# Attention queries and keys produced transposed: the weight slices stand in the array, 256 token columns move

## The chip, the core and the metric

The kernel runs on one core of one Trainium2 chip. Its metric is the device time of one execution in microseconds. The kernel before has a median of 1318.09 us over 3 runs (1317.95 to 1318.52). The engines have the names of the profile: PE is the matrix engine (PEld its weight loads), DVE the vector engine, ACT the scalar engine, POOL the general engine, SP the engine that issues DMAs.

## What is computed

A trunk of two layers over 256 tokens of width 1024, all in float32. Each layer is a half-step feed-forward part, a mixer and another half-step feed-forward part, each with a norm before and a norm after it. The mixer of layer 0 is the dilated attention that the change touches; that of layer 1 is a retention.

```python
def rms_norm(x, g):
    y = x * lax.rsqrt(jnp.mean(x * x, axis=-1, keepdims=True) + NORM_EPS)
    return y * g

# layer 0, mixer
hm = rms_norm(x, g[2])
proj = (h @ w_in).reshape(B, S, N_GROUPS, 3, H_A, DH_A)      # 1024 -> 3 groups x (q, k, v) x 16 heads x 64
for g, (window, dilation) in enumerate(((128, 1), (512, 4), (2048, 16))):
    o, lse = dilated_group(proj[:, :, g, 0], proj[:, :, g, 1], proj[:, :, g, 2], bias_g, dilation, radius)
wts = softmax(stack(lses)); o = einsum('gbsh,gbshd->bshd', wts, stack(outs))
m = o.reshape(B, S, D_A) @ w_out
x = x + rms_norm(m, g[3])
```

## The kernel before

The 256 tokens lie as two tiles t of 128. The normed input is held transposed, as `xh` and `xl` (a rounded half and the remainder), with 8 slices k of 128 features: `xh[:, k, 0:256]` is features by tokens. Each weight is likewise split into `whi` (ACT, L115) and `wlo` (DVE, L116), and a product is three matmuls (`mm3`, L182 to L184): xh by whi, xh by wlo, xl by whi. These tiles have the type fp32r. The norm's gain is multiplied into the weights when they are split; the norm's factor per token, `rstd`, is applied to the products when they leave the accumulator.

Weights stream in: SP loads 1 MB tiles `raw`, ACT and DVE split them into pieces of 1024 columns (two slices k of 512 weight columns) in a ring of six `whi` and six `wlo`, and each piece used up (`done`) triggers the split of a later one. A **unit** is 512 weight columns, so four pieces, and 48 matmuls of 512 columns on PE: for each piece, each of its two k and each t, three matmuls with the 128 tokens as the stationary operand and 512 weight columns moving. Its result, tokens by columns, fills two accumulator banks (`at` in attention; there are six banks in all).

Attention has 18 units in two rounds of 8 heads each (o = 0, 1): q and k of group 0, q and k of group 1, q and k of group 2, then v of the three groups. After a q or k unit ACT copies each accumulator to a tile `nat` and multiplies it by the norm's factor per token, which is one number per partition there (L567; `rq` is -1/8 of `rstd`). The scores need q and k with the head's features on the partitions, so `qk_store` transposes `nat` by four PE transposes of 128 columns per t into a bank `tr` (L624, tile `qkt`; two such banks) and DVE copies that to `qk` (L626 with the token order inside reversed for q, L628 for k). This work is put on the list `pend` and is emitted by `flush` after the second piece of the next unit. Score, softmax and transpose steps of a round wait in `bg`, and `work` emits two of them per piece of the v units.

Outside of two hand-ordered places the order on each engine is set by a scheduler when the program is built. PE, DVE and ACT each take their instructions strictly in that order.

## Time and profile before

| | kernel before |
|---|---|
| median of 3 runs | 1318.09 us |
| the profiled execution | 1317.18 us |
| its span (first to last instruction) | 1315.1 us |
| PE busy | 1298.9 us, 99% |
| PE weight loads busy | 1051.8 us, 80% |
| DVE busy | 864.7 us, 66% |
| ACT busy | 712.1 us, 54% |
| granted PE clock | 0.999 |

The profiled execution is 0.91 us below the median, and 2.1 us of it lie outside the span. A matmul's busy time in the trace is longer than its place in the stream, since the next one starts while it still drains. What a matmul costs is therefore read from start to start.

### The profile page before, as it was taken

How to read it: one execution, taken by the hardware profiler on the slowest of the kernel's cores; microseconds unless marked ns; L12 is line 12 of the kernel's file. 1: busy time of each engine (PE TensorE's matmuls, PEld its weight loads, DVE VectorE, ACT ScalarE, POOL GpSimd, SP SyncE). 2: the span in 40 equal slices, each digit the busy share in tenths (PEclk: the TensorE clock that was granted, in tenths of full speed). 3: DMA queues.
4: the chain of work that ended last, by engine and by line, in shares of the span. 5: the costliest groups of instructions: out<-in, count | busy, mean ns of one | idle time of the engine just before them, and what ended most of it. 6: DMA issues, size and time to landing. Idle time of an engine off the chain costs nothing.

```text
span 1315.1 us, 16640 instructions
## 1 busy us (share of the span) xinstructions
PE 1298.9 (99%) x6326; PEld 1051.8 (80%) x6326; DVE 864.7 (66%) x1541; ACT 712.1 (54%) x1103; POOL 19.4 (1%) x16
## 2 busy tenths in 40 slices
PE   8999999999999999999999999999999999999997
PEld 6878887877887778888888888877888887888886
DVE  5765547678467768765476665588787875766544
ACT  4655444566555658764455654455554545565532
POOL 1000001000000000000000000000000000000000
PEclk9999999999999999999999999999999999999999
DMA  7755467855864346554546555545454545565551
GB/s 214 235 183 192 173 212 183 203 192 147 204 179 158 129 149 227 192 192 173 184 162 227 170 189 192 192 144 185 152 175 145 176 160 192 166 202 183 172 190 64
DMA packets 129691, 235.45 MB, mean 179 GB/s; under 512 B 25019, under 2 KB 41899, under 8 KB 129612
## 3 DMA queue, kind: packets, MB, share of 16 engines
q1 hardware_dynamic: 129468, 234.14, 56.0%
q8 instruction: 49, 0.80, 0.2%
q10 hardware_dynamic: 144, 0.26, 0.1%
q14 instruction: 30, 0.25, 0.1%
HBM read 232.21 MB, written 1.12 MB: 177 GB/s over the span
## 4 chain that ended last, share of the span: by engine, by line
PE 90%; DVE 4%; DMA 3%; ACT 2%; issue 1%; SPq 0%; DVEq 0%; ACTq 0%
PE ac_f L184 12%; PE ac_f L183 12%; PE ac_f L182 12%; PE d_f L182 6%; PE d_f L184 6%; PE d_f L183 6%; PE at L182 5%; PE at L184 5%; PE at L183 5%; PE rt L184 4%; PE rt L183 4%; PE rt L182 4%; PE htr L340 1%; DMA raw<-in_ret_w_in_dram 1%; DMA raw<-in_ffn_w_gate_dram 1%; PE ptt L676 1%
## 5 line engine op out<-in xcount | busy, mean ns | idle before, releaser
L116 DVE SCALAR_TENSOR_TENSOR wlo<-raw,gcol,whi 128x512 fp32r<-128x512 f32 x596 | 417.2, 747 | 191.2 <-ACT whi L115 190.6
L115 ACT ACTIVATE whi<-raw,gcol 128x512 fp32r<-128x512 f32 x596 | 393.8, 715 | 273.2 <-PE ac_f L184 87.1
L110 DVE TENSOR_TENSOR wlo<-raw,whi 128x1024 fp32r<-128x1024 f32 x112 | 137.2, 1225 | 144.9 <-ACT whi L109 144.7
L109 ACT ACTIVATE whi<-raw 128x1024 fp32r<-128x1024 f32 x112 | 118.7, 1060 | 172.2 <-PE d_f L184 103.3
L182 PE MATMUL d_f<-whi,hhf 128*128 128x512 f32 x352 | 140.7, 400 | 0.0
L184 PE MATMUL d_f<-whi,hlf 128*128 128x512 f32 x352 | 138.8, 394 | 0.0
L183 PE MATMUL d_f<-wlo,hhf 128*128 128x512 f32 x352 | 138.2, 393 | 0.0
L182 PE MATMUL at<-whi,xh_f 128*128 128x512 f32 x276 | 111.6, 404 | 0.0
L184 PE MATMUL at<-whi,xl_f 128*128 128x512 f32 x276 | 108.3, 392 | 0.0
L183 PE MATMUL at<-wlo,xh_f 128*128 128x512 f32 x276 | 107.4, 389 | 0.0
L183 PE MATMUL rt<-wlo,xh_f 128*128 128x512 f32 x244 | 97.1, 398 | 0.0
L182 PE MATMUL rt<-whi,xh_f 128*128 128x512 f32 x244 | 96.7, 396 | 0.0
L184 PE MATMUL rt<-whi,xl_f 128*128 128x512 f32 x244 | 96.4, 395 | 0.0
L184 PEld LDWEIGHTS d_f<-whi,hlf 128*128 128x128 f32 x352 | 66.1, 188 | 17.1
L183 PEld LDWEIGHTS d_f<-wlo,hhf 128*128 128x128 f32 x352 | 66.1, 188 | 15.4
L182 PEld LDWEIGHTS d_f<-whi,hhf 128*128 128x128 f32 x352 | 66.1, 188 | 15.1
L182 PE MATMUL ac_f<-whi,xh_in 128*128 128x512 f32 x176 | 70.4, 400 | 2.2 <-ACT whi L115 1.9
L183 PE MATMUL ac_f<-wlo,xh_in 128*128 128x512 f32 x176 | 69.1, 392 | 1.2 <-DVE wlo L116 1.2
L184 PE MATMUL ac_f<-whi,xl_in 128*128 128x512 f32 x176 | 69.3, 394 | 0.0
L184 PE MATMUL ac_f<-whi,xl_at 128*128 128x512 f32 x168 | 66.2, 394 | 0.0
L182 PE MATMUL ac_f<-whi,xh_at 128*128 128x512 f32 x168 | 65.8, 393 | 0.2 <-ACT xh_at L224 0.2
L183 PE MATMUL ac_f<-wlo,xh_at 128*128 128x512 f32 x168 | 65.9, 392 | 0.0
(290 smaller groups left out, 2162.8 us busy)
## 6 DMA issues: line engine op xcount, KB each, us to landing
raw<-in_ffn_w_down_dram SPq DMA_DIRECT2D x44, 1024.0 KB, 4.9
raw<-in_ffn_w_up_dram SPq DMA_DIRECT2D x40, 1024.0 KB, 5.1
raw<-in_ffn_w_gate_dram SPq DMA_DIRECT2D x39, 1024.0 KB, 5.1
raw<-in_attn_w_in_dram SPq DMA_DIRECT2D x36, 1024.0 KB, 5.2
raw<-in_ret_w_in_dram SPq DMA_DIRECT2D x24, 1024.0 KB, 5.4
raw<-in_ret_w_in_dram SPq DMA_DIRECT2D x16, 512.0 KB, 4.6
raw<-in_ret_w_out_dram SPq DMA_DIRECT2D x8, 1024.0 KB, 4.9
raw<-in_ffn_w_gate_dram SPq DMA_DIRECT2D x10, 512.0 KB, 4.1
```

The costliest lines, as they stand in the source:

```text
L109: nc.scalar.activation(hi, raw, AF.Copy)
L110: nc.vector.tensor_tensor(out=lo, in0=raw, in1=hi.bitcast(F32), op=ALU.subtract)
L115: nc.scalar.activation(hi[:, s], raw[:, s], AF.Copy, scale=gc)
L116: nc.vector.scalar_tensor_tensor(out=lo[:, s], in0=raw[:, s], scalar=gc, in1=hi[:, s].bitcast(F32), op0=ALU.mult, op1=ALU.subtract,)
L182: mm(out, xh, wh, start=start, stop=False)
L183: mm(out, xh, wl, start=False, stop=False)
L184: mm(out, xl, wh, start=False, stop=stop)
L340: nc.tensor.transpose(tr[:, k * P : (k + 1) * P], h[:, k * P : (k + 1) * P], self.ident)
L676: self.nc.tensor.transpose(tr[:, c * P : (c + 1) * P], pr[:, c * P : (c + 1) * P], self.ident)
```

## The change

All q and k units but the very first (u = 0), 11 of 12, now run through `unit_t`. There the stationary operand is a slice of 128 weight columns, and the 256 tokens of both tiles move: for each k and each of the four slices c, three matmuls of 256 columns. The result is already transposed, features by tokens, two slices in each bank. The norm's factor is then one number per column, so `rows` builds two tiles `rowsq` and `rowsk` once, with the factor of every token in all partitions: DVE writes the factors on the diagonal of `dg`, PE multiplies by a tile of ones, DVE copies the result out. The accumulators leave through one DVE multiplication per bank by that row (with the token order reversed for q), straight into `qk`. For these units `nat`, the transposes and the copies out of `tr` are gone. The first unit stays as it was, and so do the v units.

```diff
+        self.ones = sb.tile([P, P], F32, name="ones")
+        nc.gpsimd.memset(self.ones, 1.0)
...
+    def unit_t(self, pieces, accs, quota=2):
+        mm = self.nc.tensor.matmul
+        for j, pc in enumerate(pieces):
+            hi, lo = self.ws.get(pc)
+            for kk in range(2):
+                k = 2 * j + kk
+                xh, xl = (z[:, k, 0 : 2 * P] for z in (self.xh, self.xl))
+                for c in range(4):
+                    b, a = divmod(c, 2)
+                    out = accs[b][:, a * 256 : a * 256 + 256]
+                    s = slice(kk * 512 + c * P, kk * 512 + c * P + P)
+                    mm(out, hi[:, s], xh, start=k == 0 and a == 0, stop=False, skip_group_check=True)
+                    mm(out, hi[:, s], xl, start=False, stop=False, skip_group_check=True)
+                    mm(out, lo[:, s], xh, start=False, stop=k == NK - 1, skip_group_check=True)
+            self.ws.done(pc)
+            if j == 1:
+                self.flush()
+            self.work(quota)
+
+    def rows(self, cols, name):
+        nc, sb = self.nc, self.sb
+        d = sb.tile([P, 2, P], F32, tag="dg", name=f"dg_{name}")
+        for t in range(2):
+            nc.vector.tensor_scalar(out=d[:, t, :], in0=self.ident, scalar1=cols[:, t : t + 1], scalar2=None, op0=ALU.mult)
+        tr = self.trb(f"rw_{name}")
+        nc.tensor.matmul(tr[:, : 2 * P], self.ones, d, start=True, stop=True)
+        r = sb.tile([P, 2 * P], F32, tag=f"rows{name}", name=f"rows{name}")
+        nc.vector.tensor_copy(r, tr[:, : 2 * P])
+        return r
...
+                self.pend.append(lambda rq=rq: scales.update(q=self.rows(rq, "q"), k=self.rows(self.rstd, "k")))
...
-                self.unit(pieces, accs, cols=(64, 192) if (kind == "v" and g == 2) else (0, P))
+                if kind == "v":
+                    self.unit(pieces, accs, cols=(64, 192) if g == 2 else (0, P))
+                else:
+                    self.unit_t(pieces, accs)
...
-                for t in range(2):
+                if u:
+                    for b in range(2):
+                        dst = qk[g][:, w, 2 * b : 2 * b + 2, :].rearrange("p a (r i) -> p a r i", r=4)
+                        src = accs[b].rearrange("p (a r i) -> p a r i", a=2, r=4)
+                        sc = scales[kind].rearrange("p (r i) -> p r i", r=4)
+                        if kind == "q":
+                            src, sc = src[:, :, :, ::-1], sc[:, :, ::-1]
+                        nc.vector.tensor_tensor(out=dst, in0=src, in1=sc.unsqueeze(1).to_broadcast([P, 2, 4, 64]), op=ALU.mult)
+                for t in range(2 if u == 0 else 0):
```

On PE, around the start of the second half of a k unit's pieces (unit 3), the kernel before has the transposes of the previous unit (`qkt`) between matmuls of 512 columns:

```order
L184 MATMUL at_3_1_1966<-whi79_1856,xl_f00_1586 128x512
L624 MATMUL qkt20_2007<-ident_79,nat20_1961 128x128 x4
L624 MATMUL qkt21_2013<-ident_79,nat21_1963 128x128 x4
L182 MATMUL at_3_0_1965<-whi80_1884,xh_f00_1585 128x512
L183 MATMUL at_3_0_1965<-wlo80_1885,xh_f00_1585 128x512
L184 MATMUL at_3_0_1965<-whi80_1884,xl_f00_1586 128x512
```

The changed kernel's unit 3 is 96 rows of this kind without a break, here its first ones; the operand named first after the arrow moves, the other one stands in the array:

```order
L340 MATMUL at_3_0_2061<-xh_f00_1587,whi78_1890 128x256
L341 MATMUL at_3_0_2061<-xl_f00_1588,whi78_1890 128x256
L342 MATMUL at_3_0_2061<-xh_f00_1587,wlo78_1891 128x256
L340 MATMUL at_3_0_2061<-xh_f00_1587,whi78_1890 128x256
L341 MATMUL at_3_0_2061<-xl_f00_1588,whi78_1890 128x256
L342 MATMUL at_3_0_2061<-xh_f00_1587,wlo78_1891 128x256
L340 MATMUL at_3_1_2062<-xh_f00_1587,whi78_1890 128x256
L341 MATMUL at_3_1_2062<-xl_f00_1588,whi78_1890 128x256
```

Twice as many matmuls, each half as long, have taken the place of the 48, and the transposes are gone.

On DVE, during unit 1, the kernel before has the splits `wlo` and the copies out of the transposes' banks (`qkt0` of unit 0, `qkt1` of unit 1):

```order
L553 COPY ru_1763<-rut_1760 64x1
L116 SCALAR_TENSOR_TENSOR wlo74_1688<-raw37_1652,gcol_95,whi74_1687 128x512 x2
L116 SCALAR_TENSOR_TENSOR wlo75_1731<-raw37_1652,gcol_95,whi75_1730 128x512 x2
L626 COPY qk00_1767<-qkt00_1814 128x4x128
L626 COPY qk00_1767<-qkt01_1820 128x4x128
L116 SCALAR_TENSOR_TENSOR wlo76_1789<-raw38_1685,gcol_95,whi76_1788 128x512 x2
L116 SCALAR_TENSOR_TENSOR wlo77_1807<-raw38_1685,gcol_95,whi77_1806 128x512 x2
L116 SCALAR_TENSOR_TENSOR wlo78_1839<-raw39_1736,gcol_95,whi78_1838 128x512 x2
L116 SCALAR_TENSOR_TENSOR wlo79_1857<-raw39_1736,gcol_95,whi79_1856 128x512 x2
L628 COPY qk00_1767<-qkt10_1910 128x4x128
```

The changed kernel has, at the same place:

```order
L589 COPY ru_1765<-rut_1762 64x1
L353 TENSOR_SCALAR dg_q_1840<-ident_79,rq_1758 128x128 x2
L116 SCALAR_TENSOR_TENSOR wlo74_1690<-raw37_1654,gcol_97,whi74_1689 128x512 x2
L116 SCALAR_TENSOR_TENSOR wlo75_1733<-raw37_1654,gcol_97,whi75_1732 128x512 x2
L357 COPY rowsq_1845<-rw_q_1843 128x256
L353 TENSOR_SCALAR dg_k_1847<-ident_79,rstd_f00_1589 128x128 x2
L357 COPY rowsk_1852<-rw_k_1850 128x256
L674 COPY qk00_1769<-qkt00_1854 128x4x128
L674 COPY qk00_1769<-qkt01_1860 128x4x128
L612 TENSOR_TENSOR qk00_1769<-at_1_0_1774,rowsk_1852 128x512
L612 TENSOR_TENSOR qk00_1769<-at_1_1_1775,rowsk_1852 128x512
L116 SCALAR_TENSOR_TENSOR wlo76_1803<-raw38_1687,gcol_97,whi76_1802 128x512 x2
```

The four instructions that make the rows and their two copies are new, and unit 1's accumulators now leave on DVE, ahead of the splits `wlo76` and `wlo77` of unit 2's last two pieces, which stand behind them.

## Rows read from the trace of the kernel before

**Rows 1.** The page: busy time by engine; granted PE clock by slice, tenths.

```profile
PE 1298.9 (99%) x6326; PEld 1051.8 (80%) x6326; DVE 864.7 (66%) x1541; ACT 712.1 (54%) x1103; POOL 19.4 (1%) x16
...
PEclk9999999999999999999999999999999999999999
```

**Rows 2.** Waits of PE during attention (204 to 455 us): us, times, longest.

```profile
PE xtr_f L220 <- DVE x L263: 0.3, 1, 0.3
PE rut L548 <- DVE rstd_f L211: 0.3, 1, 0.3
```

**Rows 3.** Windows, each from one block of transposes to the next: two units.

```profile
core 0: us, PE busy (x) PEld busy (x) DVE busy (x) ACT busy (x) POOL busy (x), PEclk, DMA share, GB/s
236.24:248.10 11.86, 11.86 (x59) 9.83 (x58) 4.78 (x9) 6.28 (x10) 0.00 (x0) 1.00 0.69 200
248.10:259.97 11.87, 11.87 (x59) 9.84 (x58) 8.13 (x13) 6.17 (x10) 0.00 (x0) 1.00 0.88 221
```

**Rows 4.** Timeline of PE at the first block of transposes: start us, us, instruction.

```profile
223.13 0.39 PE L183 MATMUL at<-wlo,xh_f 128*128 128x512 f32 x1
223.36 0.39 PE L184 MATMUL at<-whi,xl_f 128*128 128x512 f32 x1
223.59 1.03 PE L624 MATMUL qkt<-ident,nat 128*128 128x128 f32 x8
224.38 0.47 PE L182 MATMUL at<-whi,xh_f 128*128 128x512 f32 x1
224.70 0.39 PE L183 MATMUL at<-wlo,xh_f 128*128 128x512 f32 x1
```

**Rows 5.** Timeline of PE's weight loads at the same place.

```profile
223.14 0.19 PEld L184 LDWEIGHTS at<-whi,xl_f 128*128 128x128 f32 x1
223.37 1.02 PEld L624 LDWEIGHTS qkt<-ident,nat 128*128 128x128 f32 x8
```

**Rows 6.** Timeline of PE: the last three warm-up passes of 128 columns, plain float32.

```profile
4.27 0.50 PE L174 MATMUL warm<-ident 128*128 128x128 f32 x3
4.60 0.25 PE L176 MATMUL gtr<-ident,gr 96*128 96x96 f32 x1
```

**Rows 7.** Loads of line 174, matmuls of line 846: ns min/median/max, first, last start.

```profile
L174 PEld LDWEIGHTS warm<-ident x16: 192/333/338, 1.3 to 4.4; 128*128 128x128 f32 x16
...
L846 PE MATMUL rs<-rc x32: 379/379/483, 889.7 to 1040.6; 128*128 128x256 f32 x32
```

**Rows 8.** Timeline of PE: eight plain float32 passes of 256 columns, the retention scores.

```profile
889.69 1.99 PE L846 MATMUL rs<-rc 128*128 128x256 f32 x8 [0.52 <-ACT rc L837]
```

**Rows 9.** Timelines of PE and PEld: a matmul without a load beside it.

```profile
287.57 0.40 PE L184 MATMUL at<-whi,xl_f 128*128 128x512 f32 x1
...
287.89 0.30 PEld L644 LDWEIGHTS sc<-qk 64*128 64x128 f32 x4 [0.36 <-issue]
```

**Rows 10.** Timeline of PE in a feed-forward down projection.

```profile
159.83 0.40 PE L182 MATMUL d_f<-whi,hhf 128*128 128x512 f32 x1
...
161.23 0.40 PE L182 MATMUL d_f<-whi,hhf 128*128 128x512 f32 x1
```

**Rows 11.** Groups by line: xcount, busy us, mean ns, idle before (first four: attention).

```profile
L116 DVE SCALAR_TENSOR_TENSOR wlo<-raw,gcol,whi 128x512 fp32r<-128x512 f32 x136 | 94.4, 747 | 45.1 <-ACT whi L115 44.9
...
L567 ACT ACTIVATE nat<-at,rq 128x512 f32<-128x512 f32 x12 | 8.1, 683 | 20.4 <-PE at L184 12.8 <-DVE rq L544 7.6
L628 DVE COPY qk<-qkt 128x512 f32<-128x512 f32 x12 | 8.0, 685 | 6.5 <-PE qkt L624 6.5
...
L626 DVE COPY qk<-qkt 128x512 f32<-128x512 f32 x12 | 7.9, 686 | 10.3 <-PE qkt L624 10.3
...
L669 DVE TENSOR_SCALAR pr<-pr,den 128x384 f32<-128x384 f32 x32 | 11.9, 415 | 0.4
L824 DVE TENSOR_TENSOR m<-rt,rtab 128x512 f32<-128x512 f32 x16 | 10.3, 683 | 0.0
L680 DVE COPY PT<-ptt 128x384 f32<-128x384 f32 x16 | 8.8, 551 | 2.5 <-PE ptt L676 2.5
```

More of the change, by code (lines that the diff above doesn't have):

```diff
@@ L535, in attn @@
         rq = ru = None
+        scales = {}
         tasks_o1 = None
```

## The prediction

> **What bounds the kernel now.** I read the page's busy times first. PE is busy 99% of the span at the full granted clock, DVE 66%, ACT 54% [rows 1]. Then the waits of PE: in the whole attention stage it waited twice, 0.3 us each, both before unit 1 is well under way [rows 2]. In the windows from one block of transposes to the next PE is busy in every microsecond, while DVE and ACT idle for a third to a half [rows 3]. So the q and k units cost what PE's stream costs, and what the change adds or takes off PE moves the end by as much; the later stages start when attention is done and are as full of PE.
>
> **What PE's stream costs now.** One q or k unit with a block of transposes takes 11.87 us [rows 3]. The block: the matmul before it starts at 223.36, the second one after it at 224.70; of these 1.34 us two are ordinary matmuls (0.229 each, next sentence), so eight transposes cost 0.88 us, 0.11 each [rows 4]. The other 11.87 - 0.88 = 10.99 us over 48 matmuls make 0.229 us for one of 512 columns, which the starts confirm (223.13 to 223.36) [rows 4].
>
> **The change on PE.** It removes 11 such units with 11 such blocks: 11 x 11.87 = 130.6 us. It adds 11 x 96 = 1056 matmuls of 256 columns, each with a load of its own, at a price p that no row shows: every fp32r matmul of this kernel moves 512 columns. At p nanoseconds they cost 1.056 x p us. So p decides, and I bound it from the nearest rows.
>
> From below. Two rates limit p. Loads: three passes of plain float32 with 128x128 weights, whose loads are 0.19 long as the fp32r ones are (192 at the least; 0.19), follow one another in (4.60 - 4.27) / 3 = 0.11 us [rows 5 to 7]. The stream: eight transposes of 128 float32 columns at 0.11 each, too [rows 4]. Plain float32 passes of 256 columns take (1.99 - 0.38 - 0.10) / 7 = 0.216 (0.38 is the last one's own length, 0.10 the first one's exposed load, 483 less 379) [rows 7, 8]. So float32 doubles with its columns and has some 2 ns that don't. An fp32r matmul has twice these columns in about the same time, 229 against 216, so 256 of them should take what 128 float32 columns take or more: p is not below 109.
>
> From above. The 229 ns are 13 more than the 216 of the float32 pass. Are these 13 per matmul, or do they grow with the columns? If per matmul, p = 109 + 13 = 122. In the down projection the same shape comes every (161.23 - 159.83) / 6 = 0.233 and single starts lie 0.24 apart [rows 10]; with all of that kept per matmul p is 126, and 133 for the worst single ones. If nothing of a load could lie beside a matmul, p would be 0.109 + 0.107 (what a 0.19 load holds up beyond its neighbour, as the first pass of rows 8 shows it) = 216.
>
> What I take. Does the extra come from the load beside the matmul? The one at 287.57 has no load beside it, since the next starts at 287.89, after its place in the stream is over; it is as long as the others or longer (0.40 against 0.39) [rows 4, 9]. So the extra sits in the fp32r stream itself, and a stream's cost goes with its columns. Half of 229, with the 2 ns that don't halve, is **115.5 ns**. That is also between the nearest rows, 111 and 122.
>
> Sum on PE: 1056 x 115.5 ns = 122.0 us against 130.6, so -8.6 us. Then `rows` on PE: two float32 matmuls of 256 columns, two passes each, at 0.216 to 0.23 with the exposed load [rows 8], 0.9 us. And `rut`, which already waits 0.3 us for `rstd` [rows 2], now stands behind 5 short matmuls (0.58 us) instead of 3 long ones (0.69), so it waits 0.1 us longer. **Together -7.6 us**, and in general 1.056 x p - 129.6 (130.6 less 1.0).
>
> **The change off PE.** ACT loses 22 `nat` of 0.68 us, 15 us in all, at no gain: it waits for PE already [rows 11]. DVE loses 22 copies of 0.686 and gets 22 multiplications of 128x512 from an accumulator by a broadcast row; the rotary's have that form and take 0.683 [rows 11]. These now wait for the unit's last matmul with splits queued behind them: the `wlo` of the next unit's third and fourth piece. PE comes to the third piece 48 x 0.1155 = 5.5 us into the unit. DVE needs two multiplications and two splits, 2 x 0.69 + 2 x 0.75 = 2.9 us [rows 11]. The cover is 2.6 us; were it gone, each late microsecond would stand in each of 11 units. Nothing there touches ACT's `whi`, which moves ahead by the missing `nat`. For the rows, DVE does 4 small products, at most 0.415 each, and 2 copies, at most 0.55 [rows 11]. The second row's matmul stands 21 short matmuls (2.4 us) behind the first; DVE's copy and two products between need 1.4. The last transposes of unit 0 wait for the second row's copy (0.55), with four transposes and a matmul (0.55) beside it; so 0 to 0.2 us. SP's queue keeps its order, and POOL gets one memset at the start.
>
> **A rule against it.** The Trainium skill, page "TensorE: Matmul & The Clock Gate", section "The mechanism" with its list of what overlaps, says that a load overlaps matmuls in flight only where its row group differs. Here every load has all 128 rows. By that rule p is 216 and the time 1416.6. The trace speaks against it: the load for the matmul of 223.36 starts at 223.14, beside the one of 223.13, and matmuls still follow each other every 0.229, where 0.229 and a load's 0.107 in a row would make 0.34 [rows 4, 5]. The same page of the Trainium skill, section "Back-to-back issue gap", gives N/2.4 + 2.5 ns for a warm isolated matmul; an estimate by it is 109 ns for N = 256, by which the time would be 1303.6 us, and 216 ns for N = 512, where this trace has 229.
>
> **Rivals.**
> - Both rates run at their floor, p = 109 to 112: 1.056 x 111 - 129.6 = -12.4, so 1305.7 us. For it: the float32 passes of rows 6. Against: fp32r has never been seen at such a pace here.
> - The extra is per matmul, p = 120 to 125: at 122, -0.8, so 1317.3. The transposes' gain is given back by twice as many matmuls, and no change can be measured. For it: no row shows the extra shrink. Against: rows 9.
> - **Slower: the load becomes the bound.** In the stream of now a load of 0.19 ends 0.04 us before its matmul starts; at 0.1155 it must be handed over while its neighbour is still loading. For it: PEld is busy 9.84 of 11.87 us already [rows 3]. Against: rows 6 have such loads every 0.11. From p = 125 on the kernel is slower; at the 133 of the worst start, +10.8, so 1328.9. With loads that overlap nothing p is 216, and 1.056 x 216 - 129.6 = +98.5, so 1416.6.
> - The change isn't effective because PE isn't the bound after it: that would need waits where there are 0.6 us of them in 251 [rows 2]; I give it no chance of its own.
>
> **How the numbers follow.** The sum stands against the profiled execution, 1317.18 us; that gives 1309.6. The median of the runs is 0.91 above, so 1318.09 - 7.6 = 1310.5 is what I predict. About 0.2% of it, 2.6 us, is what a measurement can tell from no change; that is p = 120.3 below and 125.2 above. Chances: p from 112 to 120 (the forecast) 0.48, the floor 0.12, together faster 0.60; the extra per matmul 0.25, the same; the load as the bound 0.12 and loads that overlap nothing 0.03, slower 0.15. For the range I go down to 1305, p of 110.4, and up to 1321, p of 125.5; some 0.05 is left out below and 0.14 above.
>
> **What would show it.** In the changed profile, a q or k unit from 3 on lasts 96 x p with no block in it: 11.1 us if I am right, 10.7 at the floor, 11.7 if the extra stays. The starts of the 256-column matmuls give p itself, 0.115 or 0.116. PEld's busy share of these units rises to nearly all. PE's waits stay below 1 us in attention; a new one on `wlo` at a unit's third piece would mean that the evacuation has lost its cover. After attention every stage keeps its length. A p above 125 or new waits of over 5 us would make the prediction wrong.

## The result, and the profile after

The changed kernel takes 1308.43 us (median of 6 runs, 1307.12 to 1309.9) where the kernel before takes 1318.16 in the same session (6 runs, 1316.95 to 1319.95). The ratio is 0.9925, with a 95% interval of 0.9912 to 0.9937: 9.7 us faster. The profiled execution took 1308.35 us, its span is 1306.6. So the forecast, 1310.5 us and faster, held, and so did its range. Its working held less well: the price of a matmul on which it rests isn't the same in all kernels with the same code, as the runs below show.

First the page: busy time by engine, which answers [rows 1]; the granted PE clock is 0.9 or more in every slice, as it was, and 1.00 in the windows below.

```profile
PE 1290.3 (99%) x6770; PEld 1065.5 (82%) x6770; DVE 866.9 (66%) x1547; ACT 699.3 (54%) x1081; POOL 20.4 (2%) x17
...
PEclk9999999999999999999999999999999999999999
```

PE has 444 more matmuls and 8.6 us less busy time. Next the whole attention stage as one window, of before:

```profile
204.80:451.00 246.20, 245.63 (x1517) 197.19 (x1516) 168.08 (x339) 143.59 (x258) 3.71 (x3) 1.00 0.63 178
```

and of after (columns as in [rows 3]: us, then PE, PEld, DVE, ACT and POOL busy):

```profile
205.64:443.74 238.10, 236.28 (x1961) 209.64 (x1960) 170.40 (x345) 130.86 (x236) 3.71 (x3) 1.00 0.65 184
```

The stage is 8.10 us shorter. The rest of the 8.5 us by which the spans differ is code that the change doesn't touch: the stage began 0.84 us later, and what follows it took 1.2 us less. The runs of one kernel spread by about 3 us, so I read nothing into that. In the first window PE idles 0.57 us, in the second 1.82 us; of that later.

Two of the units, from the start of one to the start of the next, which answer [rows 3]:

```profile
243.19:254.07 10.88, 10.88 (x99) 10.88 (x97) 6.67 (x11) 6.22 (x11) 0.00 (x0) 1.00 0.71 219
254.07:264.95 10.88, 10.88 (x99) 10.88 (x97) 6.67 (x11) 5.32 (x9) 0.00 (x0) 1.00 0.93 241
```

A unit takes 10.88 us where it took 11.87 with its block of transposes. PE's weight loads are now busy in all of it, where they were in 9.84 of 11.87. PE's starts, which answer [rows 4]:

```profile
232.08 0.28 PE L341 MATMUL at<-xl_f,whi 128*128 128x256 f32 x1
...
234.80 0.28 PE L341 MATMUL at<-xl_f,whi 128*128 128x256 f32 x1
```

24 matmuls lie between the two, so one comes every 2.72 / 24 = 0.1133 us. **The price here is p = 113.3 ns**, and 96 of them make the 10.88 us. The loads answer [rows 5]:

```profile
231.97 0.19 PEld L341 LDWEIGHTS at<-xl_f,whi 128*128 128x128 f32 x1
232.08 0.19 PEld L342 LDWEIGHTS at<-xh_f,wlo 128*128 128x128 f32 x1
```

A load of 0.19 us starts every 0.11 us. It lies not only beside the matmul before but beside the next load as well.

PE's waits in the stage answer [rows 2] (us in all, times, longest):

```profile
PE ptt L724 <- DVE pr L717: 1.0, 1, 1.0
PE rut L584 <- DVE rstd_f L213: 0.3, 1, 0.3
PE xtr_f L222 <- DVE x L265: 0.3, 1, 0.3
```

The first is new. It belongs to the softmax steps of the first v unit, which the diff doesn't touch. PE's timeline there:

```profile
290.05 0.46 PE L698 MATMUL sc<-qk 64*64 64x64 f32 x16
291.54 0.88 PE L724 MATMUL ptt<-ident,pr 128*128 128x128 f32 x6 [1.03 <-DVE pr L717]
```

and DVE's:

```profile
289.70 0.75 DVE L637 TENSOR_SCALAR V<-at,rstd_f 128x512 f32<-128x512 f32 x1
290.36 0.15 DVE L714 RECIPROCAL den<-den 128x2 f32<-128x2 f32 x1
290.43 0.73 DVE L637 TENSOR_SCALAR V<-at,rstd_f 128x512 f32<-128x512 f32 x1
291.08 0.74 DVE L717 TENSOR_SCALAR pr<-pr,den 128x384 f32<-128x384 f32 x2
```

The probabilities `pr` have to be normalised (L717) before PE can transpose them (L724). Ahead of that on DVE stands an evacuation of V (L637) of 0.73 us whose result nobody is waiting for yet. Both evacuations now stand directly around the reciprocal. In the kernel before, one of them and two splits stood there, and PE came later (its last scores began at 292.52, the normalisation at 292.05), so that nothing waited.

Two smaller waits stand before the rows. PE:

```profile
227.23 0.28 PE L342 MATMUL at<-xh_f,wlo 128*128 128x256 f32 x1
227.60 0.67 PE L355 MATMUL rw_k<-dg_k,ones 128*128 128x256 f32 x2
```

and DVE:

```profile
223.87 2.74 DVE L116 SCALAR_TENSOR_TENSOR wlo<-raw,gcol,whi 128x512 fp32r<-128x512 f32 x4 [1.20 <-ACT whi L115]
226.64 0.42 DVE L357 COPY rowsq<-rw_q 128x256 f32<-128x256 f32 x1
226.98 0.47 DVE L353 TENSOR_SCALAR dg_k<-ident,rstd_f 128x128 f32<-128x128 f32 x2
```

0.37 us lie between the two starts on PE where a matmul takes 0.11, so 0.25 is a wait. `dg_k` is done at 227.45, since four splits, which run until 226.6, stand ahead of the copy of the first row. The transposes `qkt1` of unit 0 wait another 0.30 for the second row's copy (PE starts at 228.46 and 228.88).

**Where the 8.1 us come from**, start to start on PE over the whole stage: transposes -9.1; the matmuls of the projections -0.9, with the two small waits of 0.55 in it; the rows +0.75; the wait for `pr` +1.1. So in this kernel nearly the whole gain is the transposes that are gone. Two matmuls of 256 columns cost 226.7 ns, one of 512 before cost 229.

### The profile page after: what moved, and what is told of

Its sections match the earlier page's. It is cut to its first block, busy times and chain, and to the rows that moved or that the text cites. A ratio compares the mean times of both kernels' runs of the same rounds, so it can differ in the third digit from the quotient of the medians.

```text
span 1306.6 us, 17500 instructions
## 1 busy us (share of the span) xinstructions
PE 1290.3 (99%) x6770; PEld 1065.5 (82%) x6770; DVE 866.9 (66%) x1547; ACT 699.3 (54%) x1081; POOL 20.4 (2%) x17
## 4 chain that ended last, share of the span: by engine, by line
PE 90%; DVE 4%; DMA 3%; ACT 2%; issue 1%; SPq 0%; DVEq 0%; ACTq 0%
PE ac_f L186 12%; PE ac_f L185 12%; PE ac_f L184 12%; PE d_f L184 6%; PE d_f L186 6%; PE d_f L185 6%; PE rt L186 4%; PE rt L185 4%; PE rt L184 4%; PE at L340 2%; PE at L342 2%; PE at L341 2%; DVE wlo L116 2%; PE htr L375 1%; PE at L184 1%; PE at L186 1%
## 5 line engine op out<-in xcount | busy, mean ns | idle before, releaser
L340 PE MATMUL at<-xh_f,whi 128*128 128x256 f32 x352 | 97.6, 277 | 0.0
L342 PE MATMUL at<-xh_f,wlo 128*128 128x256 f32 x352 | 97.3, 276 | 0.0
L341 PE MATMUL at<-xl_f,whi 128*128 128x256 f32 x352 | 97.3, 276 | 0.0
L340 PEld LDWEIGHTS at<-xh_f,whi 128*128 128x128 f32 x352 | 66.1, 188 | 0.2
L341 PEld LDWEIGHTS at<-xl_f,whi 128*128 128x128 f32 x352 | 66.1, 188 | 0.1
```

What stands on the lines that cost most here:

```text
L340: mm(out, hi[:, s], xh, start=k == 0 and a == 0, stop=False, skip_group_check=True)
L341: mm(out, hi[:, s], xl, start=False, stop=False, skip_group_check=True)
L342: mm(out, lo[:, s], xh, start=False, stop=k == NK - 1, skip_group_check=True)
```

## The experiments

The runs fall in three groups: the cover and the waits on DVE, what of the change brings the gain, and what sets the price of a matmul of 256 columns.

### Is DVE's cover real?

Every evacuation by a row is done twice.

```diff
                         nc.vector.tensor_tensor(out=dst, in0=src, in1=sc.unsqueeze(1).to_broadcast([P, 2, 4, 64]), op=ALU.mult)
+                        nc.vector.tensor_tensor(out=dst, in0=src, in1=sc.unsqueeze(1).to_broadcast([P, 2, 4, 64]), op=ALU.mult)
```

> The changed kernel, with each of the 22 multiplications that take q and k out of the accumulators done twice by DVE, one behind the other: 22 x 0.69 = 15 us more for DVE, 1.4 us more between the end of a unit and the splits queued behind it. Theory C (the splits of the next unit's third and fourth piece have 2.6 us to spare): the time stays within 1.5 us of the changed kernel, and PE has no wait for wlo in attention. Rival D (DVE's evacuation is on the path already or has under 1.4 us to spare): 5 to 15 us slower, with PE waits for wlo at the third piece.

1308.88 us (4 runs, 1307.36 to 1312.12), ratio to before 0.9924 (0.9907 to 0.9941): the same as the changed kernel. The added instructions (line 613) of the k units, 12 of 22, by duration in ns (least, median, most) and first and last start; those of the q units take as long:

```profile
L613 DVE TENSOR_TENSOR qk<-at,rowsk x12: 679/684/692, 235.6 to 402.2; 128x512 f32<-128x512 f32 x12
```

PE has no wait on `wlo` in the stage, so 22 x 0.68 = 15 us more on DVE made nothing wait, and the time is the same within the runs' spread. The cover of 2.6 us per unit, out of which this takes 1.4, is real. But the units of the first round came slower in this trace, 11.30 us each, those of the second at 10.88 as in the changed kernel (a unit of each):

```profile
246.10:257.40 11.30, 11.30 (x98) 11.30 (x97) 7.87 (x13) 4.76 (x9) 0.00 (x0) 1.00 0.69 206
345.02:355.90 10.88, 10.88 (x98) 10.88 (x97) 6.81 (x11) 5.35 (x8) 0.00 (x0) 1.00 0.75 216
```

That is 117.7 ns a matmul against 113.3, with PE busy throughout. Both rounds have the second multiplication, so this alone doesn't make the difference. Of this pace more below.

### Whose is the new wait for the probabilities?

One V evacuation of the first round goes to ACT.

```diff
-                        nc.vector.tensor_scalar(out=V[:, t, :], in0=accs[t], scalar1=self.rstd[:, t : t + 1], scalar2=None, op0=ALU.mult)
+                        if t and o == 0:
+                            nc.scalar.activation(V[:, t, :], accs[t], AF.Copy, scale=self.rstd[:, t : t + 1])
+                        else:
+                            nc.vector.tensor_scalar(out=V[:, t, :], in0=accs[t], scalar1=self.rstd[:, t : t + 1], scalar2=None, op0=ALU.mult)
```

> The changed kernel, but in the first round ACT instead of DVE takes the second token tile of v of group 0 out of its accumulator. Theory O (the new wait of PE, 1.03 us for the normalised scores in front of the first block of probability transposes, comes from two 0.73 us products of DVE that the scheduler has put ahead of the normalisation): with one of them gone the wait shrinks by 0.65 to 0.75, to 0.3 to 0.4 us. Rival W (the wait is for the score itself, which the faster units make later relative to the softmax chain): the wait stays at 1.0 us. The total falls by at most 0.7 us, less than a time can show; the trace decides.

All waits of PE in the stage:

```profile
PE rut L584 <- DVE rstd_f L213: 0.3, 1, 0.3
PE xtr_f L222 <- DVE x L265: 0.3, 1, 0.3
```

The wait is gone altogether, where I expected 0.3 to 0.4 to stay; so it was the order on DVE. The time of the one run, 1308.11 us, says nothing by itself: 1 us is within the spread of the runs.

### Do the transposes bring the gain, or the other order of the operands?

From unit 1 on, each transposed unit gets eight transposes whose result nobody uses, at the place where the kernel before had them.

```diff
                     self.unit_t(pieces, accs)
+                    self.pend.append(lambda u=u: self.idle_transposes(u))
...
+    def idle_transposes(self, u):
+        for t in range(2):
+            tr = self.trb(f"idl{u}{t}")
+            for p in range(4):
+                self.nc.tensor.transpose(tr[:, p * P : (p + 1) * P], self.ident, self.ident)
```

> The changed kernel with eight PE transposes per transposed unit put back at the place where they stood before, in 11 units; they transpose the identity into the two transpose banks and nobody reads them, so the copies and the ACT evacuation don't come back. Theory G (the gain is the 88 transposes; twice as many matmuls of half the width cost the same as before within 2 us): 88 x 0.109 = 9.6 us more. In this kernel the order on DVE has the normalisation of the first scores ahead of both v products again, so the 1.0 us wait of the changed kernel goes: 8.6 us more in all, about 1317, and a ratio to the kernel before of 0.998 to 1.000. Rival H (a good part of the gain comes from the matmuls): 1314 or less.

1320.04 us (10 runs, 1318.4 to 1321.66) against 1319.24 of before, ratio 1.0006 (0.9996 to 1.0016). The gain is gone altogether. Three of these blocks in a row on PE:

```profile
239.19 1.04 PE L674 MATMUL idl<-ident 128*128 128x128 f32 x8
...
251.37 1.03 PE L674 MATMUL idl<-ident 128*128 128x128 f32 x8
...
263.15 1.03 PE L674 MATMUL idl<-ident 128*128 128x128 f32 x8
```

From the first block to the second it is 12.18 us, from the second to the third 11.78, with the same instructions. Taking off 0.88 for a block, 96 matmuls cost 117.7 ns each in the first and 113.5 in the second. In the trace the starts inside are regular, 117 to 119 throughout the one and 113 or 114 throughout the other. So part of the 11.6 us against the changed kernel (10.5 when each is held against the kernel before in its own session) is not the transposes but a slower pace, taken on after a block and kept until the next. Where a whole unit runs at 117.7, two matmuls cost 235 against 229 before: the new form is then dearer than the old one, and only the missing transposes pay for it.

### The same split without turning the operands

Every matmul of 512 columns of all stages is issued as two of 256, the tokens still standing in the array.

```diff
-        mm(out, xh, wh, start=start, stop=False)
-        mm(out, xh, wl, start=False, stop=False)
-        mm(out, xl, wh, start=False, stop=stop)
+        for a in range(2):
+            s = slice(a * 256, a * 256 + 256)
+            mm(out[:, s], xh, wh[:, s], start=start and a == 0, stop=False, skip_group_check=True)
+            mm(out[:, s], xh, wl[:, s], start=False, stop=False, skip_group_check=True)
+            mm(out[:, s], xl, wh[:, s], start=False, stop=stop, skip_group_check=True)
```

> The changed kernel, with every matmul of 512 columns that is left (4560 of them: feed-forward, retention, v units, output) issued as two of 256 columns with the same stationary operand, so each with its own load. Theory S (113.3 ns belongs to a width of 256, whichever operand stands): 226.7 ns a pair where 229 to 233 stand now; 2112 x 2.6 + 1056 x 6.6 + 432 x 2.6 + 768 x 4.8 + 192 x 6.6 ns = 18 us less, so about 1290 us. Rival T (the 113.3 belongs to weights standing and tokens moving): pairs cost 229 to 233 as now, no change, 1308 us. Rival L2 (loads or instructions become the bound at twice their number): pairs over 235, 1320 us or more.

1340.18 us (4 runs, 1339.18 to 1341.64) against 1318.91, ratio 1.0166 (1.0151 to 1.0181). In a feed-forward projection, and further on in a down projection:

```profile
120.03 0.28 PE L188 MATMUL ac_f<-whi,xl_in 128*128 128x256 f32 x1
...
121.45 0.28 PE L188 MATMUL ac_f<-whi,xl_in 128*128 128x256 f32 x1
...
149.93 0.28 PE L188 MATMUL d_f<-whi,hlf 128*128 128x256 f32 x1
...
150.65 0.28 PE L188 MATMUL d_f<-whi,hlf 128*128 128x256 f32 x1
```

1.42 / 12 = 118 ns and 0.72 / 6 = 120 ns. Two halves cost 236 to 240 ns where one whole cost 229 to 233. If a matmul's cost went with its columns, the split would be free. It isn't. In the same trace the attention units, with the weights standing, stayed at 10.88 us, so 113.3 ns; in this kernel the two forms differ.

### What a matmul costs at each width

A measuring stretch after the warm-up: 16 matmuls of each width in a row, operands of no meaning (line 198; line 202 with weights of 64 columns, whose loads are shorter).

```diff
...
+            for n in (512, 64, 128, 192, 256, 320, 384, 448, 512):
+                for i in range(16):
+                    c = (i % 4) * P
+                    mm(pb[:, :n], idr[:, c : c + P], idr[:, :n], start=True, stop=True)
+            for n in (128, 256):
+                for i in range(16):
+                    c = (i % 4) * P
+                    mm(pb[:64, :n], idr[:, c : c + 64], idr[:, :n], start=True, stop=True)
...
```

> The changed kernel with a measuring stretch put behind the warm-up matmuls, whose results nobody reads: fp32r matmuls with 128x128 weights and a new load each, 16 in a row of each width 64, 128, 192, 256, 320, 384, 448 and 512 columns, then the same with 64-column weights at widths 128 and 256, then plain float32 at 64, 128 and 256. The whole kernel gets about 20 to 30 us longer by it. Theory S (the stream decides: a column costs 0.443 ns, so 256 columns 113): starts every 113 ns at 256, 142 at 320, 170 at 384, 198 at 448, 227 to 229 at 512; below 256 the pace of the loads shows, and it is lower than 113: 107 to 110 at 64, 128 and 192; with 64-column weights 113 at 256 and under 90 at 128. Theory L (the load decides: 113 ns is the pace of fp32r loads): 113 at 64, 128 and 192 as well, and with 64-column weights, whose loads are shorter, 256 columns fall to 107 to 109. Theory F (a fixed 13 to 16 ns per fp32r matmul, 0.417 ns per column): 120 to 122 at 256 and 67 or the load's pace at 128; it is nearly out already.

Timelines of PE, each inside one width (start us, us from the first start to the last end):

```profile
19.64 2.36 PE L198 MATMUL probe<-idr 128*128 128x320 f32 x15
29.79 1.98 PE L198 MATMUL probe<-idr 128*128 128x512 f32 x8
31.60 1.06 PE L202 MATMUL probe<-idr 128*64 128x128 f32 x15
33.03 1.52 PE L202 MATMUL probe<-idr 128*64 128x256 f32 x12
```

The medians of the matmuls' own lengths in the four are 309, 389, 222 and 276 ns. The stretch less the last one's own length, over the count less one: 320 columns (2.36 - 0.309) / 14 = 146.5 ns, 512 columns 227.3; with short loads 128 columns 59.9 and 256 columns 113.1. With 128-column weights, 64 and 128 columns came every 112 ns, the pace of the loads. Those of 192 and 256 fell into a stretch of half the granted clock (below) and say nothing here.

With short loads a column costs (113.1 - 59.9) / 128 = 0.416 ns, and 113.1 - 106.4 = 6.7 ns are left per matmul. With full loads it is (227.3 - 146.5) / 192 = 0.42 per column, and 12 to 14 ns are left (384 columns, at 173 by their starts, lie on this line, 448, at 207, another 7 above it). So there is an extra **per matmul**, twice as large where a full load lies beside it. A cost that only goes with the columns would put 320 columns at 142 from the 227 of 512. By this line 256 columns with full loads cost 146.5 - 64 x 0.42 = 120.

### 120, 118 or 113: what chooses the pace?

Stretches of 256 columns in three arrangements, weights standing or tokens standing, the same slice again or another one each time, with the vector engines quiet:

```diff
...
+            for i in range(24):
+                mm(pb[:, :256], xh[:, i % 2, :P], wh[:, :256], start=True, stop=True)
+            for i in range(24):
+                mm(pb[:, :256], wh[:, 512 * (i % 2) : 512 * (i % 2) + P], xh[:, 0, :256], start=True, stop=True)
```

> The changed kernel with another measuring stretch behind the warm-up, its results unread. All operands lie at the places that the kernel's own have (tokens in tiles of 320-column slices, weights in tiles of 512-column slices), and DVE, ACT and mostly the DMA engines are at rest beside it. In this order: 24 matmuls with tokens standing and 512 weight columns moving; 48 with weights standing and 256 token columns moving; 48 with tokens standing and 256 weight columns moving; 24 of the last kind with the same moved slice each time; 24 of the second kind with the same moved slice. In the kernels with all engines at work the second kind has come every 113.3 ns, the third (matmuls issued as halves) every 117 to 121 and the first every 229 to 233. Theory P (the operands' places and roles make the difference): 229 or more, 113.3, 117 to 118 here as well. Theory Q (traffic beside it slows what moves out of the weight ring, which ACT and DVE write): 226.7, 113.3, 113.3 here.

```profile
25.56 3.04 PE L215 MATMUL probe<-pwC,pxA 128*128 128x256 f32 x24
```

(3.04 - 0.28) / 23 = 120 ns, and the same in all the other arrangements. Neither theory holds: which operand stands makes no difference in this stretch, and the pace is the 120 of the line, while the units of the same trace came at 113.3.

Next, 12 blocks of 36 matmuls with an interruption after each: four transposes (line 207), one matmul of 512 columns, or a short one.

```diff
...
+            for b in range(12):
+                for i in range(36):
+                    mm(o, (wl if i % 3 == 2 else wh)[:, s], (xl if i % 3 == 1 else xh)[:, b % 4, :256], start=True, stop=True)
+                if b < 4:
+                    for i in range(4):
+                        nc.tensor.transpose(pb[:, i * P : i * P + P], self.ident, self.ident)
+                elif b < 8:
+                    mm(pb, xh[:, 0, :P], wh[:, :512], start=True, stop=True)
+                else:
+                    mm(pb[:64, :P], xh[:, 0, :64], wh[:, :P], start=True, stop=True)
```

> The changed kernel with a measuring stretch after the warm-up: 24 ordinary 512-column matmuls, then 12 blocks of 36 matmuls of 256 columns (weights standing, the unit's order of hi, hi, lo and of two halves of one bank), with one interruption after each block: four 128-column float32 transposes after blocks 1 to 4, one 512-column matmul after blocks 5 to 8, one matmul with 64-column weights and 128 columns after blocks 9 to 12. The question is what chooses between the paces of 113, 117 to 118 and 120 ns per matmul that the earlier runs showed. Theory K (the kind of the interruption chooses): blocks that follow the same kind have the same pace, within 1 ns, and kinds differ. Theory H (the pace is chosen anew at each restart, by an alignment that no instruction shows): blocks after the same kind differ among themselves, each steady within itself, and among 12 blocks at least two of the paces appear. Theory N (nothing is chosen by interruptions; the place in the program or its data set it): all 12 blocks have one pace.

```profile
12.14 0.28 PE L204 MATMUL probe<-pxA,pwC 128*128 128x256 f32 x1
...
16.33 0.28 PE L204 MATMUL probe<-pxA,pwC 128*128 128x256 f32 x1
```

The first block: 4.19 / 35 = 120 ns. All 12 blocks come to 120 on average once they run (two of them in a cycle of 117, 121, 120, 124, 118). Interruptions alone don't choose, not of any of these three kinds: theory N, against K and H. The units of the same trace came at 113.3.

Three more stretches took what else differs between a measuring stretch and a unit. First the data and the way of writing: nearly empty against dense operands, overwriting one half bank against accumulating in two banks in turn, and blocks with 64-column weights between.

```diff
...
+            def blk(d, acc=True, m=P, n=36):
+                for i in range(n):
+                    q = i // 3 % 4
+                    o = pb2[q // 2][:m, (q % 2) * 256 : (q % 2) * 256 + 256] if acc else pb[:m, :256]
...
+                    mm(o, (wl if i % 3 == 2 else wh)[:, s : s + m], (xl if i % 3 == 1 else xh)[:, 2 * d + i // 12 % 2, :256], start=st, stop=sp, skip_group_check=acc)
+            blk(0)
+            blk(1)
+            blk(1, acc=False)
+            blk(1, m=64)
...
```

> The changed kernel with a measuring stretch of 256-column fp32r matmuls in blocks of 36, weights standing: (1) operands almost all zero, written as a unit writes (accumulating, two banks in turn); (2) the same with dense non-zero operands; (3) dense, but always the same half bank and overwriting; (4) dense, weights of 64 columns; (5) as 2; (6) as 1; (7) as 1 with weights of 64 columns; (8) as 1; six 512-column matmuls; (9) and (10) as 2, 36 and 96 matmuls. In the measuring stretches so far the matmuls of 256 columns came every 120 ns, with the operands zero and the same half bank overwritten; in the changed kernel's attention every 113 ns. Theory A (accumulating in two banks makes 113): blocks 1, 2, 5, 6, 8 to 10 at 113, block 3 at 120. Theory D (the data make it): dense blocks at 113 and zero ones at 120. Theory E (what stood before the block makes it, and the pace stays): blocks 5 and 8, which follow the short loads, keep the 113 of these, blocks 1 and 2 stay at 120. Theory R (none of these): all blocks with 128-column weights at 120, the ones with 64-column weights at 113.

The block with 64-column weights, and later one with 128-column weights in the unit's own form:

```profile
27.07 0.28 PE L214 MATMUL probe<-pxA,pwC 128*64 128x256 f32 x1
...
28.43 0.28 PE L214 MATMUL probe<-pxA,pwC 128*64 128x256 f32 x1
...
44.12 0.28 PE L214 MATMUL probd<-pxA,pwC 128*128 128x256 f32 x1
...
46.03 0.28 PE L214 MATMUL probd<-pxB,pwC 128*128 128x256 f32 x1
```

1.36 / 12 = 113 ns and 1.91 / 16 = 119.5, 120 by all starts of the block. It was theory R: 120 in every block with full loads, 113 in every block with short ones. What stood before left no trace either. The units of this trace came at 113.3 once more.

Then the operands' places, which a unit has in the ring of the splits and in the normed input's tile:

```diff
...
+        for key, tags in (("x", ("xh", "xl")), ("a", "AB")):
+            X[key] = [sb.tile([P, NK, XC], F32R, tag=t, name=f"p{t}") for t in tags]
...
+        for key, tags in (("r", ("whi", "wlo")), ("c", ("C0", "C1")), ("s", ("whi", "wlo"))):
...
+            blk("r", "x")
+            blk("r", "a")
+            blk("c", "x")
+            blk("c", "a")
...
```

> The changed kernel with a measuring stretch of seven blocks of 48 matmuls of 256 columns, all as a unit writes them (dense operands, accumulating, two banks in turn), which differ only in where the operands lie on chip: weights in the ring of the split weights or in the place that the earlier stretches used, tokens in the place of the normed input or in the one that the earlier stretches used. Order: ring with input's place; ring with old place; old weights' place with input's place; both old; ring with input's place; another slot of the ring with input's place, twice. The four earlier kinds of blocks in the old places all came every 120 ns, where the kernel's own units come every 113. Theory P (the operands' places set the pace): the block with both old places at 120, and 113 where the weights (or the tokens) lie where the kernel has them. Theory R (not the places): all at 120, and what makes 113 in the units is something that these stretches still lack, such as the work of the other engines and of the DMAs beside it.

```profile
25.30:30.90 5.60, 5.60 (x49) 5.60 (x48) 0.00 (x0) 0.00 (x0) 0.00 (x0) 1.00 0.01 3
```

That is the first block, with both operands allocated under the tags of the unit's own tiles: 120 ns by its starts, as in the other six. Last, ACT and DVE at work beside it:

```diff
...
+        for i in range(24):
+            o = slice(i % 2 * 512, i % 2 * 512 + 512)
+            nc.scalar.activation(da[:, o], W["c"][0][:, 512:], AF.Copy)
+            nc.vector.tensor_copy(db[:, o], W["c"][1][:, 512:])
...
+            for i in range(9):
+                blk("r", "x")
```

> The changed kernel with a measuring stretch of nine equal blocks of 48 matmuls of 256 columns, as a unit writes them and with the operands in the units' own places; beside the first ones ACT and DVE each copy 24 times 128x512 without a pause, as they are busy beside the units, the later blocks run with both engines idle. All quiet stretches so far settled at 120 ns per matmul, the kernel's own units at 113. Theory T (work on ACT and DVE moves the stream to the faster pace): 113 in the blocks with copies beside them, and it either stays or goes back to 120 afterwards. Theory R (not that either): 120 from the first to the last block; then what gives the units 113 stays open.

```profile
25.20:28.80 3.60, 3.60 (x32) 3.60 (x31) 3.60 (x12) 3.60 (x9) 0.00 (x0) 1.00 0.02 5
62.40:66.00 3.60, 3.60 (x32) 3.60 (x31) 0.00 (x0) 0.00 (x0) 0.00 (x0) 1.00 0.00 0
```

As many matmuls with DVE and ACT busy throughout as with both idle, again at 120.

These last two runs show more than their stretches do. The kernel's own attention units, whose code is that of the changed kernel, came every 120 ns in them, too. One unit, and the whole attention stage, of the run on places:

```profile
285.60:297.12 11.52, 11.52 (x98) 11.52 (x97) 6.68 (x11) 4.75 (x8) 0.00 (x0) 1.00 0.73 219
258.73:502.34 243.61, 242.48 (x1962) 216.35 (x1961) 170.78 (x345) 130.59 (x236) 3.73 (x3) 1.00 0.61 180
```

In the run with copies a unit takes 11.52 us as well and the stage 244.03. So what a unit has and a quiet stretch lacks, such as other engines and DMAs at work, signals to other engines and new pieces, isn't enough to bring 113. And where the units run at 120 themselves, a stretch at 120 says nothing against theory P or T: places are not excluded. Only these two stretches allocate under the tags of `whi`, `wlo`, `xh` and `xl`, ahead of the kernel itself; whether the kernel's own tiles lie elsewhere for that, no trace shows. In these two traces matmuls of 512 columns in the feed-forward parts and down projections came every 227 ns, where the changed kernel has 229 to 233.

**What brings the units to 113 stays open.** Units of the same code came at 113.3 in the changed kernel and six others, at 117.7 in the first round and 113.3 in the second in three (the evacuation done twice, the stretch of all widths, and the last version below), at 120 throughout in two, and with the transposes back the pace changes at a block. Beside units at 113.3 in the same trace, stretches stayed at 120 whichever operand stood, with either kind of data, one bank or two, and after each kind of interruption. Each kernel was profiled once, so whether another execution of it would show another pace is not known.

### Can the gain be had elsewhere?

In the feed-forward parts, gate and up projections are also transposed on PE (`htr`) before they go on. Here all their units but the first two are changed in the same way, and the transposes there are gone as well.

```diff
...
-            else:
-                self.unit(pieces, accs)
+            elif u == 1:
+                self.unit(pieces, accs)
+            else:
+                self.unit_t(pieces, accs)
...
```

> The changed kernel, with the same step taken in the four feed-forward parts: all gate and up units but the first two of each (9 of 11) have the weights standing and the 256 tokens moving, the result is already transposed for the down projection, DVE multiplies by the row of the norm's factors, and 144 of 176 transposes are gone. Theory S/T (113.3 ns for this arrangement wherever it is used): the q and k units' gain repeats: 144 x 0.109 = 15.7 us, 1728 x (229.5 - 226.7) ns = 4.8 us, less four times the rows at 0.6 us; together -18 us, about 1290 us, a ratio to the kernel before of about 0.979. Rival D2 (DVE, which gets two more products of 0.69 us per unit pair's bank, becomes late): PE waits for wlo or whi in the feed-forward units, 1296 to 1310.

1305.72 us (4 runs, 1301.71 to 1307.98), ratio to before 0.9896 (0.9877 to 0.9916). That is 2.7 us less than the changed kernel in the medians (3.8 when each is held against the kernel before in its own session), far short of what I expected. PE's two longest waits, neither of which the changed kernel has at this length:

```profile
PE ac_f L184 <- ACT whi L115: 2.4, 1, 2.4
PE rw_f L355 <- DVE dg_f L353: 1.7, 1, 1.7
```

Two starts on PE in the first feed-forward part:

```profile
40.01 0.28 PE L340 MATMUL ac_f<-xh_in,whi 128*128 128x256 f32 x1
...
41.42 0.28 PE L340 MATMUL ac_f<-xh_in,whi 128*128 128x256 f32 x1
```

1.41 / 12 = 117.5 ns, and 117 on average over the 3456 matmuls of this form, longer gaps left out: 234 for a pair where one of 512 columns cost 229 to 231. I had counted on 113. On 1728 pairs that is 13 us, the larger part of what is missing; the wait at the rows (1.7 us) is another.

The same with the V evacuation on ACT:

> The version with the feed-forward units transposed as well, and one of the two V evacuations of the first round on ACT, which took the wait for the probabilities away in an earlier run. If each wait counts for itself, 1.1 us less than the feed-forward version alone (1305.7), so about 1304.6. If the matmuls' pace after each interruption decides more than a wait of 1 us, the time is anywhere from 1302 to 1308 and the two versions can't be told apart.

1306.0 us (4 runs, 1303.08 to 1306.62), ratio 0.99 (0.9883 to 0.9916), so the two can't be told apart. In this one the matmuls of the attention units came every 115.4 ns on average, at 117.7 in the first round and 113.3 in the second, though nothing of their code differs. Both versions are faster than the kernel before; against the changed kernel a gain is not shown: some 2 to 4 us are about the spread of the runs, and the intervals of the ratios overlap.

## Why the prediction was right, and where it was not

**What bounds it: right.** PE is busy in each microsecond of a unit, before and after. The change is worth what it takes off PE, less the waits that it adds.

**The price p: 2 ns off, and the reason for it false.** I took 115.5 for p, because the extra "sits in the fp32r stream itself, and a stream's cost goes with its columns". It measured 113.3. But the stretches show an extra per matmul, 12 to 14 ns at 512 and 320 columns and 13 at 256 (120), and the split into halves shows it in the kernel: 236 to 240 for two, 229 to 233 for one. In its form the rival "the extra is per matmul, p = 120 to 125" was right for most streams. At 120 the general sum gives 1.056 x 120 - 129.6 = -2.9 us, at the edge of what can be told from no change. Two kernels show that this would have been so: where the units ran at 120, the attention stage took 243.61 and 244.03 us against 246.20 before, so 2.6 and 2.2 less, with the same transposes gone. That the attention units ran at 113.3, with an extra of only 7, carried the forecast, and what gave them this pace is open. So a false reason led to a nearly right number, and that it was nearly right is luck.

The step that failed is the one on the matmul at 287.57 [rows 9]. I took from its length (0.40 against 0.39) that a missing load saves nothing. A length is not the distance to the next start, as the 0.39 against 0.229 of the same rows show. In the measuring stretches shorter loads save 6.7 ns a matmul from start to start. The trace of before had no row that could show that.

**Loads as the bound: not so, but near.** A load of 0.19 us can start every 112 ns, and the units' matmuls come every 113.3. The chance of slower, 0.15, rested on p above 125, which no steady stretch at the full clock shows. The rule of the Trainium skill ("TensorE: Matmul & The Clock Gate", "The mechanism") by which p would have been 216 is refuted for this form: full-row loads lie beside full-row matmuls at 113.

**The transposes: right.** 0.88 us a block made 9.7, start to start over the stage it is 9.1, and putting blocks back took the whole gain away, in part by the pace that came with them.

**The extras: 2.8 us where I had 1.0.** The rows cost 0.75 of the forecast 0.9. Their copy stood behind four splits on DVE where I had reckoned with a free DVE ("DVE's copy and two products between need 1.4"), and that made waits of 0.25 and 0.30. The wait of 1.1 us for `pr` was in no step: I had compared the order of instructions only around the units, while the scheduler also moved the V evacuations in front of the softmax.

**The sum.** At 113.3 the general sum is 1.056 x 113.3 - 129.6 = -10.0; with 1.1 and 0.55 of waits not foreseen, -8.3; the stage measured -8.1. The forecast was -7.6, by two errors against each other: 2.3 too little gain in p, 1.65 too few waits.

**The cover: right.** No wait on `wlo` at any unit's third piece, nor with the evacuation done twice. **A unit of 11.1, 10.7 or 11.7 us:** it was 10.88, nearest the middle between the first two. **Waits below 1 us:** 1.0 plus the two small ones, just missed.

## What to carry to other kernels

Where a product is needed transposed, count first the transposes on PE that go away: here they are nearly the whole gain. A matmul of half the width is not half the price: 113 to 120 ns for 256 columns against 227 to 233 for 512, so what is gained must be more than this. At 113 the attention stage gained 8.1 us and at 120 some 2.4, with the same code, so read the pace from the trace of the kernel that will run. After a change in one stage, read the order on the other engines some units on as well, since the scheduler may let an evacuation that nobody waits for pass an instruction that PE needs next.

## What the runs showed of the hardware

- Streams of equal fp32r matmuls, each with a full load, ran at one of several paces that hold for tens of microseconds to the nanosecond: 113.3, 117.7 or 120 ns at 256 columns. After a break a stream settles within some five uneven starts (in the changed kernel, behind `rut`, 117, 117, 123 and 118 ns, then 113 and 114), and the units' code ran at 113.3 in one kernel, partly at 117.7 in others and at 120 throughout in two.
- fp32r loads of 128x128, 0.19 us long, overlap each other: one every 112 ns.
- In units at an even pace the recorded length of the loads goes with it: 187 or 188 ns at 113.3, 192 at 120, and at 117.7 one load in three has 192 (the evacuation done twice). A unit of the changed kernel, and one of the run on places:

```profile
L341 PEld LDWEIGHTS at<-xl_f,whi x32: 187/188/188, 243.2 to 253.7; 128*128 128x128 f32 x32
L383 PEld LDWEIGHTS at<-xl_f,whi x29: 192/192/192, 284.9 to 295.0; 128*128 128x128 f32 x29
```

  Which of the two makes the other isn't shown, and in the halves with the tokens standing it isn't so: they came at 118 with loads of 188.
- In the first measuring stretch the granted clock fell to half, the 1.2 GHz level, right behind matmuls of 64 and 128 columns that came at the loads' pace, with PE busy throughout. The windows of the 128-column and the 192-column matmuls (the clock is the number after POOL):

```profile
10.80:12.50 1.70, 1.70 (x18) 1.70 (x17) 0.00 (x0) 0.00 (x0) 0.00 (x0) 1.00 1.06 210
13.00:15.90 2.90, 2.90 (x16) 2.90 (x15) 0.00 (x0) 0.00 (x0) 0.00 (x0) 0.50 1.03 352
```

  At the lower level 192 and 256 columns both came every 213 ns, so something other than the columns, perhaps the loads, sets that pace. 512 columns came every 0.43 us at it (the changed kernel's start, at a granted clock of 0.50: 10.62, 11.05, 11.47 and 11.90), and 512 columns at 1.2 GHz are 0.427: of the extra per matmul that the full clock has, none shows.
